# Keeping the last 32 tokens' gates on the chip and re-pacing the gathers, one-hots and u blocks of a PEER block

## The chip, the core and the metric

The kernel runs on one NeuronCore of a Trainium2 chip. The engines work side by side, each through its own instruction queue in program order, and wait for one another by semaphores: PE multiplies matrices, DVE (VectorE) and ACT (ScalarE) do elementwise work, POOL (GpSimd) does elementwise work and issues gathers, SP issues DMA. The metric is device microseconds (us) of one launch, lower is better.

## The reference, cut to what matters

```python
h2  = rmsnorm(x, g_ffn)                                  # 512 tokens of 1024
q   = (h2 @ w_q).reshape(T, 8, 2, 128)                   # 8 heads, two halves
s   = einsum('thpc,hpkc->thpk', q, sub_keys)             # 128 keys for each half
top_s, top_i = top_k(s, 16)                              # best 16 of each half
cand = top_s[:, :, 0, :, None] + top_s[:, :, 1, None, :] # their sums
fin_s, pos = top_k(cand, 16);  idx = 128 * i + j of the winners
gates = softmax(fin_s)
act = gelu(einsum('thkd,td->thk', expert_u[idx], h2))    # 128 experts of each token
x   = x + einsum('thk,thkd->td', gates * act, expert_v[idx])
out = rmsnorm(x, g_final)
```

Ahead of this stand a token mixer (projections, pooling, a short convolution) and its residual, which the change doesn't touch.

## The kernel before, in words

All matrix products are float32 split into a high and a low half and three products (`mm3`, lines 57 to 60). A high half is a cast on ACT (`split`, line 54; `u_high`, line 430; `v_high`, line 826), a low half is a subtraction on DVE or POOL (lines 55, 434, 830).

- **Two ways to the experts.** 320 of the 512 tokens (TU) go densely: all 16384 experts are multiplied, as 128 blocks of 128 experts. The other 192 tokens gather their 128 experts' rows from HBM. Half a tile of tokens (TM = 64) gathers only u; a last tile of 128 tokens gathers u and v.
- **A u block** (`u_tick`, or its parts written out): load 128 experts' u (`ur`, SP), high half on ACT (`u_high`, for the block two further on), low half (`u_low`, POOL or DVE, the same block), 24 matmuls into `b` (`u_mm`), gelu on ACT into `a` (`u_act`, line 451), and for the first 75 blocks a store to HBM (`Ad`). Blocks run in all stages: in norm (U_NORM = 2), in routing (U_HEAD, by head, and U_GATE = 10 after the heads), in the build (48), after it (U_END = 4) and the rest in the v stage.
- **Routing.** For each of 8 heads: queries on PE, top 16 on DVE (`best_keys`), sums of candidates on POOL (`candidates`), top 16 of the sums (`best_sums`), one-hot comparisons (`best_pairs`), their products on POOL (`pair_mults`), sums (`pair_keys`). It ends in `key` and `gate`, transposed on PE into columns `cols` in the middle of a u block.
- **The build.** The gate matrix of every dense token (128 x 128 keys) is a product of two one-hot matrices. 48 iterations of 8 tokens: in each, `one_hots(n + 2)` and `one_hots(n + 3)` compare on DVE for the groups of 4 tokens of the next iteration; then come a u block, the copies of older results from PSUM to `stage` (`to_stage`, ACT), the low half `u_low(i + 2)` on DVE, the one-hot matmuls of groups n and n + 1, and after each group some gathered rows (`gather`). Of the one-hots, `oi` carries no gate and ACT multiplies it in (4 activations, line 769) for even groups; for odd groups DVE does comparison and gate in 4 `tensor_scalar` (line 773). A full stage of 32 tokens (2 MB) is written to HBM (`Gd`), 12 times.
- **Rows.** The gathers form one list (`plan`): 64 u rows of the half tile, then the last tile's u and v rows by chunks of 16. `gather(want, more)` uses rows up to number want on DVE (lines 711 and 718) and has POOL issue at most `more` further ones, at most LAG = 4 ahead. After the 16th u row of a chunk come a gelu on ACT and a product on POOL (line 716), and POOL's later gathers stand behind that product. R_BUILD = 0.93 is the number of rows for each group in the build.
- **After the build.** `a_load` and `g_load` bring activations and gates back from HBM, 4 expert blocks of gates at a time (`gt`). Four u blocks (k = 0 to 3) run; `weigh(0)` stands in the third. `weigh(i)` multiplies activations and gates on DVE (line 852) and splits them (`wH`, `wL`).
- **The v stage.** For each i, `v_mm(i)` (line 864) multiplies 128 experts' v with the weights, while `weigh(i + 1)`, the v halves of i + 2 and some rows go on; from i = 74 on each iteration has a u block too. The rows are spread by costs (1.25 without a u block, 3.4 with one) to end some iterations before the last.

The order in each queue is that of the code (`manual_schedule`).

Of the kernel before, what the change touches and what calls it, by code (L numbers as in the profile page):

```python
# [8 lines left out]
F32 = mybir.dt.float32  # L9
# [7 lines left out]
P = 128  # L17
D = 1024
# [5 lines left out]
NK = 128  # L24
# [6 lines left out]
TD = KD * P  # L31

TM = 64
TU = TD - TM

U_NORM, U_HEAD, U_GATE, U_END = 2, (1, 1, 2, 1, 2, 1, 2, 1), 10, 4

R_BUILD = 0.93

TG, IG = 32, 4  # L40

# [6 lines left out]
def block_kernel(ctx: ExitStack, tc: tile.TileContext, io, out, dbg=None):  # L48
    nc = tc.nc
# [14 lines left out]
    def bank(i, dt=F32):  # L64
        return psum.tile([P, 512], dt, tag=f"b{i}", name=f"b{i}")
# [7 lines left out]
    keep = ctx.enter_context(tc.tile_pool(name="keep", bufs=1))  # L73
# [78 lines left out]
    def norm(tb, g, dst=None):  # L152

        xg = dst if dst is not None else wpool.tile([P, D], F32, tag="xg", name="xg")
        st = rms_sum([x1[:, tb]], [xg])
        rms_sqrt(st)
        nc.vector.scalar_tensor_tensor(xg, x1[:, tb], rms_inv(st)[0], g, op0=ALU.mult, op1=ALU.mult)
        return xg
# [147 lines left out]
    for hf in range(2):  # L306
# [11 lines left out]
        for e in range(2):  # L318
# [6 lines left out]
            g = hf * 2 + e  # L325
# [7 lines left out]
        for e in range(2):  # L333
            zb = z_chunk(wb, e)
            p = fpool.tile([P, T], F32, tag="p", name="yb", bufs=2)
# [10 lines left out]
    for hf in range(4):  # L346
# [14 lines left out]
        for e in range(2):  # L361
# [4 lines left out]
            t = fpool.tile([P, T], F32, tag="s", name="t", bufs=2)  # L366
# [4 lines left out]

    nc.scalar.activation(warm, warm, AF.Sqrt)
    hn = keep.tile([P, NT - KD, D], F32, name="hn")
    hm = keep.tile([P, D], F32, name="hm") if TM else None
    h2H = keep.tile([P, DC, T], F32R, tag="hH", name="h2H")
    h2L = keep.tile([P, DC, T], F32R, tag="hL", name="h2L")

# [36 lines left out]
    n_ahead = U_NORM + sum(U_HEAD) + U_GATE + TD // 8 + U_END  # L414
    assert TM in (0, P // 2)
    dram = ctx.enter_context(tc.tile_pool(name="dram", bufs=1, space=bass.MemoryType.DRAM))
    Gd = dram.tile([TD // TG, P, NK, TG], F32, name="Gd")
    Ad = dram.tile([n_ahead, P, TU], F32, name="Ad")
    raws, us, hid = {}, {}, {}
    nu = [0]  # L420
# [1 line left out]
    def u_load(i):  # L422
        if i < NK:
            raws[i] = upool.tile([P, DC, P], F32, tag=f"ur{i % 3}", name="ur", bufs=1)
            nc.sync.dma_start(raws[i], io["expert_ut"][i])

    def u_high(i):
        if i < NK:
            us[i] = [upool.tile([P, DC, P], F32R, tag=f"u{x}{i % 3}", name=f"u{x}", bufs=1) for x in "HL"]
            nc.scalar.copy(us[i][0], raws[i])  # L430

    def u_low(i, eng):
        if i < NK:
            eng.tensor_tensor(us[i][1], raws.pop(i), f(us[i][0]), ALU.subtract)  # L434
# [5 lines left out]
    def u_mm(i, half=None):  # L440
        o = bank(i % 2)
        uH, uL = us.pop(i)
        for c in range(DC):
            if c == DC // 2 and half is not None:
                half()
            mm3(o[:, :TU], uH[:, c], uL[:, c], h2H[:, c, :TU], h2L[:, c, :TU], c == 0, c == DC - 1)
        return o

    def u_act(i, o):
        a = upool.tile([P, TU], F32, tag="a", name="a", bufs=3)  # L450
        nc.scalar.activation(a, o[:, :TU], AF.Gelu)  # L451
        if i < n_ahead:
            nc.scalar.dma_start(Ad[i], a)
        else:
            hid[i] = a

    def u_tick(n=1, eng=nc.gpsimd, half=None):
        for _ in range(n):
            i = nu[0]
            nu[0] += 1  # L460
            u_load(i + 3)
            u_high(i + 2)
            if eng is not None:
                u_low(i + 2, eng)
            u_act(i, u_mm(i, half))
# [16 lines left out]
    add_x(NT - 1, 1, o)  # L482
    norm_T(NT - 2, xgs[NT - 2], h2H, h2L, (bank(6), bank(7)))
    norm(NT - 1, gb2, hn[:, 0])
    u_tick()
    norm_T(NT - 1, hn[:, 0], h2H, h2L, (bank(6), bank(7)))
    u_tick(U_NORM - 1)
    if TM:

        for q in range(2):  # L490
# [99 lines left out]
    def pair_mults(h, eng=nc.gpsimd):  # L590
        full = [P, NT, TOPK, TOPK]
        for s in range(2):
            eq, tf = eqs[h, s]
            eng.tensor_tensor(eq, eq, tf[:, :, None, :].to_broadcast(full), ALU.mult)
# [20 lines left out]
            pair_mults(h - 1)  # L615
        w = w_next
    best_keys(q1, H - 1, 1)
    u_tick(2)
    pair_mults(H - 2)
    candidates(H - 1)  # L620
    u_tick()
# [12 lines left out]
    nc.vector.tensor_tensor(gate, gate, zs[:, :, :, None].to_broadcast([P, NT, H, TOPK]), ALU.mult)  # L634
    pair_mults(H - 1, nc.vector)
    pair_keys(H - 1)
    u_tick(U_GATE - 5)


    cols = [upool.tile([P, KD, P], F32, name=f"col{s}", bufs=1) for s in range(3)]  # L640
# [80 lines left out]
    def gather(want, more):  # L721

        gather_use(min(want, n_issue[0]))
        gather_issue(min(n_done[0] + LAG, n_issue[0] + more))
# [1 line left out]

    vpool = tc.alloc_tile_pool(name="vpool", bufs=3, reuse_waits="tile")
    opool = tc.alloc_tile_pool(name="opool", bufs=3, reuse_waits="tile")
    spool = tc.alloc_tile_pool(name="spool", bufs=2, side="right", reuse_waits="tile")
    vraw, vs, gts, ws, abs_ = {}, {}, {}, {}, {}  # L730

    def v_load(i):
# [4 lines left out]
    built, stages = {}, {}  # L737

    def to_stage(n):

        t1 = 4 * n % TG
        if t1 == 0:
            stages[0] = spool.tile([P, NK, TG], F32, tag="stage", name="stage")
        stage = stages[0]
        nc.scalar.copy(stage[:, :, t1:t1 + 4], built.pop(n).rearrange("p (t i) -> p i t", t=4))
        if t1 + 4 == TG:
            for q in range(2):
                ks = slice(q * 64, q * 64 + 64)
                nc.scalar.dma_start(Gd[4 * n // TG, :, ks], stage[:, ks])
# [3 lines left out]
    def one_hots(n):  # L753

        if n >= TD // 4:
            return
        tb, t0 = divmod(4 * n, P)
        oi, oj = (opool.tile([P, 4, P], F32, tag=x, name=x, bufs=4) for x in ("oi", "oj"))
        full = [P, 4, P]

        def compare(o, c):
            nc.vector.tensor_tensor(o, iota[:, None, :].to_broadcast(full), c[:, tb, t0:t0 + 4][:, :, None].to_broadcast(full),
                                    ALU.is_equal)

        compare(oi, cols[0])
        if n % 2 == 0:
            compare(oj, cols[1])
            for t in range(4):
                nc.scalar.activation(oi[:, t], oi[:, t], AF.Copy, scale=cols[2][:, tb, t0 + t:t0 + t + 1])
        else:  # L770
            for t in range(4):
                c1, c2 = (c[:, tb, t0 + t:t0 + t + 1] for c in cols[1:])
                nc.vector.tensor_scalar(oj[:, t], iota, c1, c2, op0=ALU.is_equal, op1=ALU.mult)
        hot[n] = (oi, oj)
# [5 lines left out]
    for n in range(0, TD // 4, 2):  # L780
        left = TD // 4 - n
        if TM and left == TM // 4 + 6:

            assert n_done[0] >= TM
            ms_ = mdots[:, TM:2 * TM]
            nc.scalar.activation(ms_, ms_, AF.Gelu)
            nc.vector.tensor_tensor(ms_, ms_, mgate, ALU.mult)
        if TM and left == TM // 4 + 2:

            b = bank(2 + (n + 2) % 6)  # L790
            for q in range(2):
                nc.tensor.matmul(b[:, :TM], mdots[:, (1 - q) * TM:(1 - q) * TM + P], ident[:, q * TM:(q + 1) * TM],
                                 start=q == 0, stop=q == 1)
            nc.scalar.copy(cols[2][:, KD - 1, P - TM:], b[:, :TM])
        one_hots(n + 2)
        one_hots(n + 3)
        i = nu[0]
        nu[0] += 1
        u_load(i + 3)
        u_high(i + 2)  # L800
        if n:
            to_stage(n - 2)
            to_stage(n - 1)
        u_act(i, u_mm(i))
        u_low(i + 2, nc.vector)
        if 24 <= left < 30:
            v_load((28 - left) // 2)
        for g in (n, n + 1):
            oi, oj = hot.pop(g)
            b = bank(2 + g % 6)  # L810
            for t in range(4):
                nc.tensor.matmul(b[:, t * P:(t + 1) * P], oj[:, t], oi[:, t], start=True, stop=True)
            built[g] = b
            gather(int((g + 1) * R_BUILD), 2)
    to_stage(TD // 4 - 2)
    to_stage(TD // 4 - 1)
    opool.release()
# [3 lines left out]
    epool = tc.alloc_tile_pool(name="epool", bufs=2, reuse_waits="tile")  # L821
# [10 lines left out]
    def g_load(i):  # L832
        if i < NK:
            if i % IG == 0:
                gt = epool.tile([P, TD // TG, IG, TG], F32, tag="gt", name="gt")
                nc.sync.dma_start(gt.rearrange("p n i t -> p n (i t)"),
                                  Gd[:, :, i:i + IG, :].rearrange("n j i t -> j n (i t)"))
                for k in range(IG):
                    gts[i + k] = gt[:, :, k]

    def a_load(i):
        if i < n_ahead:
            abs_[i] = epool.tile([P, TU], F32, tag="ab", name="ab", bufs=3)
            nc.sync.dma_start(abs_[i], Ad[i])
# [24 lines left out]
            v_part(i, tb)  # L869
        del ws[i], vs[i]  # L870

    gfin = epool.tile([P, D], F32, name="gfin", bufs=1)

    def add_acc(tb, hf):
        cs = slice(hf * 512, (hf + 1) * 512)
# [24 lines left out]
    acc = [[bank(2 + 2 * tb + hf) for hf in range(2)] for tb in range(KD)]  # L900
    a_load(0)
    a_load(1)
    for k in range(U_END):
        u_tick(1, nc.vector)
        gather(n_issue[0], 2)
        if k == 0:
            v_high(0)
            v_low(0)
        if k == 1:
            g_load(0)  # L910
            v_high(1)
            v_low(1)
        if k == U_END - 2:
            weigh(0)
# [58 lines left out]
    vpool.release()  # L973
    gpool.release()
    upool.release()


# ---- launch: one core; inputs as the reference has them, without the leading axis of one layer
# [38 lines left out]
```

## Time and profile before

| what | value |
|---|---|
| time, 3 runs | median 1573.53 us (1570.72 to 1574.1) |
| the profiled execution's own time | 1573.27 us |
| its span (first to last instruction) | 1571.5 us |
| busy: PE, DVE, ACT, POOL | 1483.9 (94%), 1241.7 (79%), 625.8 (40%), 715.7 (46%) us |
| mean granted clock of TensorE | 0.980 |
| DMA | 419.57 MB, 267 GB/s over the span |

The span is 1.8 us shorter than the time of the same execution; sums over spans are therefore added to 1573.27 us. The stages by the trace: mixer to 293, norm to about 312, routing to 503, build 508 to 800, the four u blocks and the first v blocks to 850, v stage without u blocks to 1157, with them to 1535, then the last norm. Times in rows are us from the span's start.

### The profile page before, as it was taken

What the parts mean: (1) busy time and instruction counts of PE and PEld (TensorE: products, weight loads), DVE (VectorE), ACT (ScalarE), POOL (GpSimd) and SP (SyncE); (2) the same over time, 40 slices, a digit from 0 to 9 for tenths busy, and PEclk for the clock granted to TensorE, in tenths of its full rate; (3) what the DMA queues carried; (4) which work ended last, traced back from release to release, by engine and by line L of the source; (5) the groups of instructions that cost most, each with busy time, mean ns of one, the idle gap of its engine ahead of it and who ended that gap; (6) DMA issues with size and microseconds to landing.
All of it is one profiled execution on the core that took longest, in us unless ns stands there. A gap on an engine that the chain in (4) does not pass through costs nothing. (4 is left out here: it accounts for less than half of the span.)

```text
span 1571.5 us, 22106 instructions
## 1 busy us (share of the span) xinstructions
PE 1483.9 (94%) x7953; PEld 1304.4 (83%) x7953; DVE 1241.7 (79%) x2455; ACT 625.8 (40%) x1016; POOL 715.7 (46%) x448
## 2 busy tenths in 40 slices
PE   8999999899997989888967999999999999999997
PEld 6788888788897988888966887887789999999996
DVE  6832334559999999999977888887788989898985
ACT  4222222433334555555542333333334333333344
POOL 3433222247777433333344444443355666566620
PEclk9999999999998999999998999999999999999999
DMA  5222234422224999999899999999999999999971
GB/s 181 88 87 82 92 108 161 153 92 107 80 93 140 346 337 374 333 366 381 324 392 350 342 358 338 360 352 319 332 366 336 370 378 361 374 364 356 360 282 67
DMA packets 167452, 419.57 MB, mean 267 GB/s; under 512 B 13744, under 2 KB 84144, under 8 KB 160688
## 3 DMA queue, kind: packets, MB, share of 16 engines
q1 hardware_dynamic: 106944, 212.92, 38.4%
q0 software_dynamic: 46144, 167.80, 28.2%
q10 hardware_dynamic: 14256, 37.46, 6.4%
q8 instruction: 62, 1.02, 0.2%
q14 instruction: 46, 0.38, 0.1%
HBM read 377.99 MB, written 39.55 MB: 266 GB/s over the span
## 5 line engine op out<-in xcount | busy, mean ns | idle before, releaser
L58 PE MATMUL b<-h2H,uH 128*128 128x320 f32 x1024 | 327.3, 320 | 29.8 <-ACT a L451 29.5
L60 PE MATMUL b<-h2H,uL 128*128 128x320 f32 x1024 | 321.2, 314 | 12.1 <-POOL uL L434 6.6
L59 PE MATMUL b<-h2L,uH 128*128 128x320 f32 x1024 | 321.0, 314 | 1.0 <-DVE h2L L55 1.0
L699 POOL DMA_INDIRECT gr<-in_expert_u,gidx x128 | 204.2, 1595 | 187.7 <-DVE dots L711 108.4
L699 POOL DMA_INDIRECT gr<-in_expert_v,gidx x128 | 189.8, 1483 | 144.9 <-DVE x L718 102.2
L864 PE MATMUL b<-vH,wH 128*128 128x512 f32 x768 | 242.0, 396 | 13.8 <-ACT wH L54 13.8
L864 PE MATMUL b<-vL,wH 128*128 128x512 f32 x768 | 239.2, 392 | 0.0
L864 PE MATMUL b<-vH,wL 128*128 128x512 f32 x768 | 239.0, 392 | 0.0
L58 PEld LDWEIGHTS b<-h2H,uH 128*128 128x128 f32 x1024 | 197.3, 193 | 36.6 <-ACT a L451 34.0
L60 PEld LDWEIGHTS b<-h2H,uL 128*128 128x128 f32 x1024 | 196.8, 192 | 13.0 <-POOL uL L434 6.8
L59 PEld LDWEIGHTS b<-h2L,uH 128*128 128x128 f32 x1024 | 197.0, 192 | 3.2 <-DVE h2L L55 1.2
L54 ACT CAST wH<-gt 128x384 fp32r<-128x384 f32 x128 | 65.7, 513 | 300.7 <-DVE gt L852 296.5
L864 PEld LDWEIGHTS b<-vH,wH 128*128 128x128 f32 x768 | 142.7, 190 | 44.9 <-ACT wH L54 19.7
L718 DVE SCALAR_TENSOR_TENSOR x<-gr,dots,x 128x1024 f32<-128x1024 f32 x128 | 164.0, 1281 | 15.0 <-DMA gr<-in_expert_v,gidx 13.2
L864 PEld LDWEIGHTS b<-vL,wH 128*128 128x128 f32 x768 | 145.5, 189 | 31.2
L864 PEld LDWEIGHTS b<-vH,wL 128*128 128x128 f32 x768 | 145.4, 189 | 30.7
L830 DVE TENSOR_TENSOR vL<-vr,vH 128x1024 fp32r<-128x1024 f32 x128 | 156.5, 1223 | 16.5 <-ACT vH L826 13.7
L826 ACT CAST vH<-vr 128x1024 fp32r<-128x1024 f32 x128 | 134.6, 1051 | 81.2 <-PE b L864 74.8
L711 DVE CUSTOM_DVE_ANT_0 gr<-gr,hn 128x1024 f32<-128x1024 f32 x128 | 152.3, 1219 | 9.2 <-DMA gr<-in_expert_u,gidx 9.1
L55 POOL TENSOR_TENSOR wl<-raw,wh 128x2048 fp32r<-128x2048 f32 (+1 forms) x21 | 79.3, 3775 | 156.0 <-ACT wh L54 156.0
L699 POOL DMA_INDIRECT gr<-in_expert_u,midx x64 | 82.4, 1288 | 124.9 <-DVE mdots L711 111.9
L430 ACT CAST uH<-ur 128x1024 fp32r<-128x1024 f32 x128 | 133.1, 1040 | 14.9 <-DMA ur<-in_expert_ut 9.4
(215 smaller groups left out, 2526.8 us busy)
## 6 DMA issues: line engine op xcount, KB each, us to landing
ur<-in_expert_ut SPq DMA_DIRECT2D x128, 512.0 KB, 7.1
vr<-in_expert_v SPq DMA_DIRECT2D x128, 512.0 KB, 6.7
Gd<-stage ACTq DMA_DIRECT2D x24, 1024.0 KB, 8.9
gt<-Gd SPq DMA_DIRECT2D x32, 768.0 KB, 10.0
raw<-in_w_in SPq DMA_DIRECT2D x15, 1024.0 KB, 4.8
Ad<-a ACTq DMA_DIRECT2D x75, 160.0 KB, 6.0
ab<-Ad SPq DMA_DIRECT2D x75, 160.0 KB, 7.9
raw<-in_w_q SPq DMA_DIRECT2D x8, 1024.0 KB, 8.7
```

Source lines behind the costliest of these rows:

```text
L54: nc.scalar.copy(Hd, src)
L55: (nc.gpsimd if pool else nc.vector).tensor_tensor(Ld, src, f(Hd), ALU.subtract)
L58: nc.tensor.matmul(o, lh, rh, start=first, stop=False)
L59: nc.tensor.matmul(o, lh, rl, start=False, stop=False)
L60: nc.tensor.matmul(o, ll, rh, start=False, stop=last)
L430: nc.scalar.copy(us[i][0], raws[i])
L699: nc.gpsimd.indirect_dma_start(out=r, out_offset=None, in_=io["expert_u" if kind == "u" else "expert_v"], in_offset=bass.IndirectOffsetOnA ...
L711: nc.vector.tensor_tensor_reduce(out=r, in0=r, in1=src, op0=ALU.mult, op1=ALU.add, scale=1.0, scalar=0.0, accum_out=dst)
L718: nc.vector.scalar_tensor_tensor(x1[:, KD + g], r, dots[:, g, k:k + 1], x1[:, KD + g], op0=ALU.mult, op1=ALU.add)
L826: nc.scalar.copy(vs[i][0], vraw[i])
L830: nc.vector.tensor_tensor(vs[i][1], vraw.pop(i), f(vs[i][0]), ALU.subtract)
L864: nc.tensor.matmul(acc[tb][hf], lw[:, ts], rw[:, hf * 512:(hf + 1) * 512], start=i == 0 and rw is vH and lw is wH, stop=last and i == NK - 1)
```

## The change

1. Odd groups n with n % 4 = 1 now also leave the gate to ACT (two comparisons on DVE, 4 activations on ACT). Only n % 4 = 3 keeps the 4 `tensor_scalar`.
2. From row 64 on the build takes rows at R_LATE = 0.4 for each group, not 0.93.
3. The last stage of 32 tokens (of 12) isn't written to HBM. It stays in its own pool to the end; `g_load` loads 11 chunks (704 KB, not 768) and ACT copies the twelfth. The final norm's weights take the memory of `hm`.
4. `g_load(0)` stands ahead of the four u blocks, not in the second.
5. In norm, both u blocks stand ahead of the last tile's transposes. After the heads, 4 blocks stand ahead of `pair_mults(H - 2)` and `candidates(H - 1)`, not 2, and 3 at the end, not 5.

```diff
-R_BUILD = 0.93
+R_BUILD, R_LATE = 0.93, 0.4
...
-    Gd = dram.tile([TD // TG, P, NK, TG], F32, name="Gd")
+    Gd = dram.tile([TD // TG - 1, P, NK, TG], F32, name="Gd")
...
     norm(NT - 1, gb2, hn[:, 0])
-    u_tick()
+    u_tick(U_NORM)
     norm_T(NT - 1, hn[:, 0], h2H, h2L, (bank(6), bank(7)))
-    u_tick(U_NORM - 1)
...
     best_keys(q1, H - 1, 1)
-    u_tick(2)
+    u_tick(4)
     pair_mults(H - 2)
     candidates(H - 1)
     u_tick()
...
-    u_tick(U_GATE - 5)
+    u_tick(U_GATE - 7)
...
-        if t1 + 4 == TG:
+        if t1 + 4 == TG and 4 * n // TG < NG - 1:
             for q in range(2):
                 ks = slice(q * 64, q * 64 + 64)
                 nc.scalar.dma_start(Gd[4 * n // TG, :, ks], stage[:, ks])
...
-        if n % 2 == 0:
+        if n % 4 != 3:
             compare(oj, cols[1])
             for t in range(4):
                 nc.scalar.activation(oi[:, t], oi[:, t], AF.Copy, scale=cols[2][:, tb, t0 + t:t0 + t + 1])
...
-            gather(int((g + 1) * R_BUILD), 2)
+            gather(int(min((g + 1) * R_BUILD, TM + max(0, g + 1 - TM / R_BUILD) * R_LATE)), 2)
...
-                gt = epool.tile([P, TD // TG, IG, TG], F32, tag="gt", name="gt")
-                nc.sync.dma_start(gt.rearrange("p n i t -> p n (i t)"),
+                gt = epool.tile([P, NG, IG, TG], F32, tag="gt", name="gt")
+                nc.sync.dma_start(gt[:, :NG - 1].rearrange("p n i t -> p n (i t)"),
                                   Gd[:, :, i:i + IG, :].rearrange("n j i t -> j n (i t)"))
+                nc.scalar.copy(gt[:, NG - 1], stages[0][:, i:i + IG])
...
     a_load(1)
+    g_load(0)
     for k in range(U_END):
         u_tick(1, nc.vector)
         gather(n_issue[0], 2)
...
         if k == 1:
-            g_load(0)
```

**ACT in the build, two iterations before.** `oi` scaled by line 769 belongs to a group's one-hots, `uH` is the high half of the u block two further on, `b` to `stage` the copies from PSUM.

```order
L769 ACTIVATE oi<-oi,col_4159 128x128 x4
L430 CAST uH<-ur 128x1024
L745 COPY stage<-b_4846 128x128x4
L745 COPY stage<-b_4854 128x128x4
L451 ACTIVATE a<-b_4885 128x320
L453 DMA Ad<-a 128x320
L769 ACTIVATE oi<-oi,col_4159 128x128 x4
```

Now, at the same place:

```order
L771 ACTIVATE oi<-oi,col_4159 128x128 x8
L430 CAST uH<-ur 128x1024
L747 COPY stage<-b_4854 128x128x4
L747 COPY stage<-b_4862 128x128x4
L451 ACTIVATE a<-b_4894 128x320
L453 DMA Ad<-a 128x320
L771 ACTIVATE oi<-oi,col_4159 128x128 x4
```

In every second iteration 8 activations stand ahead of the cast `uH` where 4 stood; in the other ones nothing moved.

**DVE in the build now**, in such an iteration: the low half `uL` reads that `uH`, and the rows (line 710 now, 711 before) stand behind it.

```order
L764 TENSOR_TENSOR oi<-iota,col_4157 128x512
L764 TENSOR_TENSOR oj<-iota,col_4158 128x512
L764 TENSOR_TENSOR oi<-iota,col_4157 128x512
L764 TENSOR_TENSOR oj<-iota,col_4158 128x512
L434 TENSOR_TENSOR uL<-ur,uH 128x1024
L710 ISA gr,mdots<-gr,hm 128x1024
```

Before, the fourth of these was `L773 TENSOR_SCALAR oj<-iota,col_4158,col_4159 128x128 x4`; `uL` stands at the same place behind it.

**SP after the build, before and now**: the loads of activations (`ab`), of u (`ur`) and of gates (`gt`).

```order
L844 DMA ab<-Ad 128x320 x2
L425 DMA ur<-in_expert_ut 128x1024 x2
L836 DMA gt<-Gd 128x12x128
L425 DMA ur<-in_expert_ut 128x1024 x2
L916 DMA gfin<-in_g_final 128x1024
```

```order
L847 DMA ab<-Ad 128x320 x2
L838 DMA gt<-Gd 128x11x128
L425 DMA ur<-in_expert_ut 128x1024 x4
L919 DMA gfin<-in_g_final 128x1024
```

The gate load moved ahead of the first two u loads. On POOL, after the heads, the low halves `uL` that stand ahead of `pair_mults(H - 2)` and `candidates(H - 1)` are two more, and two fewer stand behind them.

## Rows read from the trace of the kernel before

**Rows 1.** Stages: window, length, busy PE, PEld, DVE, ACT, POOL, clock, DMA, GB/s

```profile
312.00:503.00 191.00, 179.64 (x1007) 160.83 (x1006) 169.16 (x879) 67.57 (x100) 131.81 (x81) 0.97 0.29 103
508.00:800.00 292.00, 263.67 (x1907) 259.35 (x1905) 288.81 (x549) 165.05 (x375) 117.23 (x91) 0.98 0.95 352
...
851.00:1157.00 306.00, 300.03 (x1307) 244.76 (x1307) 248.04 (x330) 113.34 (x148) 129.35 (x80) 0.99 0.97 342
1157.00:1535.00 378.00, 378.00 (x2084) 342.45 (x2083) 332.11 (x403) 144.48 (x208) 214.20 (x140) 1.00 0.95 353
```

**Rows 2.** Waits of PE: total us, times, longest

```profile
PE b L58 <- ACT a L451: 29.5, 23, 5.9
...
PE b L60 <- POOL uL L434: 6.6, 1, 6.6
```

**Rows 3.** Timeline of DVE, one build iteration (start, us, operation)

```profile
597.19 0.69 DVE L762 TENSOR_TENSOR oi<-iota,col 128x512 f32<-128x512 f32 x1
...
599.02 1.10 DVE L773 TENSOR_SCALAR oj<-iota,col,col 128x128 f32<-128x128 f32 x4
600.15 1.23 DVE L434 TENSOR_TENSOR uL<-ur,uH 128x1024 fp32r<-128x1024 f32 x1
601.30 1.22 DVE L711 CUSTOM_DVE_ANT_0 gr<-gr,hm 128x1024 f32<-128x1024 f32 x1
```

**Rows 4.** Timeline of ACT, the same iteration

```profile
597.91 1.28 ACT L769 ACTIVATE oi<-oi,col 128x128 f32<-128x128 f32 x4 [2.89 <-DVE oi L762]
599.09 1.03 ACT L430 CAST uH<-ur 128x1024 fp32r<-128x1024 f32 x1
```

**Rows 5.** Timeline of PE: first and last group of the last build iteration

```profile
794.61 0.41 PE L58 MATMUL b<-h2H,uH 128*128 128x320 f32 x1
...
798.24 1.97 PE L812 MATMUL b<-oi,oj 128*128 128x128 f32 x16
```

**Rows 6.** Timelines of DVE, POOL and PE in norm

```profile
300.32 2.27 DVE L147 TENSOR_TENSOR st<-st 128x1 f32<-128x1 f32 x1
...
300.22 2.34 POOL L434 TENSOR_TENSOR uL<-ur,uH 128x1024 fp32r<-128x1024 f32 x1
...
304.43 1.94 PE L166 MATMUL b<-ident,hn 128*128 128x128 f32 x8 [3.88 <-DVE hn L157]
```

**Rows 7.** Timelines of POOL and DVE at the end of routing

```profile
468.81 5.53 POOL L594 TENSOR_TENSOR eq<-eq,tf 128x1024 f32<-128x1024 f32 x2 [3.94 <-DVE eq L584]
474.30 1.17 POOL L551 TENSOR_TENSOR cand<-tv 128x128 f32<-128x128 f32 x4
...
475.50 0.67 DVE L514 MAX8 fv<-cand 128x8 f32<-128x80 f32 x4 [1.02 <-POOL cand L551]
...
495.92 4.56 DVE L594 TENSOR_TENSOR eq<-eq,tf 128x1024 f32<-128x1024 f32 x2
```

**Rows 8.** Timelines after the build: ACT, SP, PE, DVE, POOL

```profile
806.07 1.06 ACT L430 CAST uH<-ur 128x1024 fp32r<-128x1024 f32 x1 [0.89 <-ACT stage L745]
817.45 1.05 ACT L430 CAST uH<-ur 128x1024 fp32r<-128x1024 f32 x1 [8.54 <-DMA ur<-in_expert_ut]
...
814.86 0.38 SPq L836 DMA_DIRECT2D gt<-Gd  x1
...
818.88 0.63 PE L58 MATMUL b<-h2H,uH 128*128 128x320 f32 x1 [5.91 <-ACT a L451]
...
828.85 1.21 DVE L711 CUSTOM_DVE_ANT_0 gr<-gr,hn 128x1024 f32<-128x1024 f32 x1
...
831.50 1.05 POOL L699 DMA_INDIRECT gr<-in_expert_v,gidx  x1
...
838.10 1.28 DVE L718 SCALAR_TENSOR_TENSOR x<-gr,dots,x 128x1024 f32<-128x1024 f32 x1 [3.65 <-DMA gr<-in_expert_v,gidx]
...
843.35 1.22 PE L864 MATMUL b<-vH,wH 128*128 128x512 f32 x2 [5.30 <-ACT wH L54]
```

**Rows 9.** Granted clock while the second v block starts (columns as in rows 1)

```profile
843.00:849.00 6.00, 5.65 (x13) 4.46 (x14) 5.05 (x6) 1.76 (x3) 1.84 (x2) 0.51 0.98 328
```

More of the change, by code (lines that the diff above doesn't have):

```diff
@@ L373, in block_kernel @@
     hn = keep.tile([P, NT - KD, D], F32, name="hn")
-    hm = keep.tile([P, D], F32, name="hm") if TM else None
+    hm = keep.tile([P, D], F32, tag="hm", name="hm")
     h2H = keep.tile([P, DC, T], F32R, tag="hH", name="h2H")
@@ L728, in block_kernel @@
     opool = tc.alloc_tile_pool(name="opool", bufs=3, reuse_waits="tile")
-    spool = tc.alloc_tile_pool(name="spool", bufs=2, side="right", reuse_waits="tile")
+    lpool = tc.alloc_tile_pool(name="lpool", bufs=1, side="right", reuse_waits="tile")
+    spool = tc.alloc_tile_pool(name="spool", bufs=1, side="right", reuse_waits="tile")
+    NG = TD // TG
     vraw, vs, gts, ws, abs_ = {}, {}, {}, {}, {}
@@ L742, in to_stage @@
         if t1 == 0:
-            stages[0] = spool.tile([P, NK, TG], F32, tag="stage", name="stage")
+            stages[0] = (lpool if (4 * n // TG) % 2 == (NG - 1) % 2 else spool).tile([P, NK, TG], F32, tag="stage", name="stage")
         stage = stages[0]
         nc.scalar.copy(stage[:, :, t1:t1 + 4], built.pop(n).rearrange("p (t i) -> p i t", t=4))
-        if t1 + 4 == TG:
+        if t1 + 4 == TG and 4 * n // TG < NG - 1:
             for q in range(2):
@@ L870, in v_mm @@
         del ws[i], vs[i]
-    gfin = epool.tile([P, D], F32, name="gfin", bufs=1)
+    gfin = keep.tile([P, D], F32, tag="hm", name="gfin")
     def add_acc(tb, hf):
@@ L975, in block_kernel @@
     upool.release()
+    lpool.release()
 _SHAPES = {
```

## The prediction

> **What bounds the kernel now.** I read the busy times by stage first [rows 1]. The reader is to see which engine has no slack where. In routing and above all in the build it is DVE: 288.8 of the build's 292 us, while PE has 263.7. In the v stage it is PE: 300.0 of 306 us, then 378.0 of 378, with DVE at 81% and 88%. So a microsecond of DVE counts in full in the build, and in the v stage only when DVE is late by more than its slack. The waits of PE [rows 2] say the same: most of its idle time, 29.5 us, is a wait for an ACT gelu, and ACT itself is behind DVE.
>
> Then I read one build iteration on DVE and ACT side by side [rows 3, 4], because the change touches both. DVE compares from 597.19; three comparisons take 1.83 us (0.61 each), the four gated ones 1.13 (599.02 to 600.15). ACT starts its 4 gate activations at 597.91, as soon as the first comparison is there, and after 1.18 us casts `uH` (599.09 to 600.12). DVE's `uL` starts at 600.15. So two things end together there: DVE's own comparisons (600.13) and ACT's cast (600.12). `uL` needs both, and the rows stand behind it. After `uL` the next thing starts 1.15 us later, and a row costs 1.15 as well.
>
> **The change, part by part.** All times below are in the frame of the trace of before.
>
> *Odd groups to ACT.* DVE replaces 1.13 us by one comparison of 0.61 and saves 0.52. But ACT has a second group of 4 activations ahead of the cast: 1.18 us more, by the same row. The cast then ends at 599.09 + 1.18 + 1.03 = 601.30, and `uL` can't start before 601.33, where DVE would have been ready at 599.6. DVE stands for about 1.7 us, and the rows behind it with it. Net: +1.18 us in each such iteration. ACT can't start earlier, since its first activation waits for DVE's first comparison of the same iteration (2.89 us idle ahead of it). The affected iterations are n = 2, 6, ... 90: 23. Sum +27.1 us; between 23 (if 0.18 of it hides) and 29.4 (if the full 1.28 of a group counts).
>
> *Fewer rows late.* At the end of iteration n = 90 (92 groups) before wants 0.93 * 92 = 85 rows, the change 64 + 0.4 * (92 - 68.8) = 73. That takes 12 * 1.15 = 13.8 us from DVE. Does PE allow it? One iteration of PE lasts 3.63 us of u block and 1.97 of one-hots [rows 5], 5.6, a pair 11.2. DVE's late pair is 2.98 + 1.15 and 4.16 + 1.15 with 0.8 rows each, 11.3. So DVE still decides, barely. Build in sum: +27.1 - 13.8 = **+13.3 us** (+9 to +16).
>
> *Norm.* PE stands 3.88 us ahead of the last transposes [rows 6], waiting for `hn`. The second u block, 3.63 us, now fills this. But its low half on POOL now comes right behind the one that ends at 302.56. The rows show what that does: a 1-element DVE product took 2.27 us, from 300.32 to the very end of POOL's operation. Two operations that make `hn` stand behind it, and would wait some 2.3 us once more. So of at most 4.7 us (the gap and about a microsecond of clock behind it), none to all is won: **-2**. Routing starts that much earlier, and as DVE bounds routing it ends that much earlier.
>
> *Four u blocks ahead of `pair_mults`.* POOL idled for 3.94 us ahead of `pair_mults` [rows 7]. Two more low halves of 2.34 us don't fit in there, and the second must wait for a cast that follows another block's gelu: I count until about 471.8, so `pair_mults`, 468.81 before, start 3 us later, and `cand` too, at about 477.3. DVE, which waited 1.02 us for it, waits about 4. Behind it two fewer low halves run against DVE's products; each can stretch one by 2.2 us (two products that take 2.3 us alone took 4.56 at 495.92), but the moved ones now meet the comparisons ahead of `pair_mults`. I take **+2.8** (0 to +5). PE's wait of 6.6 us [rows 2] goes, but wins nothing: the ten blocks are the same ten, and PE now waits longer for the keys.
>
> *After the build.* This is where the load of gates hurts now [rows 8]. Let T0 = 800.2 be the end of the last one-hots (798.24 + 1.97). The gate load stands at 814.86, behind a 2 MB write; an u load came 8.54 us late, PE waited 5.91 at 818.88, and the second v block starts at T0 + 43.1, at a granted clock of 0.51 [rows 9], the 1.2 GHz level: about 2.9 us more. In all 46.
> Now: no write, so `uH` of k = 0 (806.07, T0 + 5.9) comes at about T0 + 5.3 and its `uL` at + 6.4. DVE has from there: that `uL`, 4 rows, a v half, `uL`, 2 rows: 9 * 1.15 = 10.4, end at + 16.7. The second of these 2 rows is number 80, the 16th of a chunk. Behind it stand gelu, product and two gathers, which the next two rows need ahead of `weigh(0)`. That is the stall that before has at 828.85: row, product, gather at 831.50, next row at 838.10, 8.1 us after the chunk's last row ended; with two rows some 11. So `weigh(0)` comes at + 27.8, the first v block at about + 29, with a cold start of 7 us; the second at + 36. Gain **-10** (-5 to -16: less if the rows' gathers are late, most if they aren't).
>
> *V stage.* 15 more rows are left, 15 * 1.22 = 18 us of DVE, in 684 us where DVE has 104 us free: hidden but for iterations with two rows, which get more frequent; PE loses there 6 of 306 us now. One ACT copy for every 4 blocks (0.3 us by the activations of [rows 4]) is hidden: ACT is busy for 38%. The DMA gets 15 * 0.5 MB more and 30 * 64 KB less. I take **+2** (-1 to +7).
>
> Sum: 13.3 - 2 + 2.8 - 10 + 2 = +6.1 us. The profiled execution took 1573.27 us, 0.3 below the median of the runs, so **1579 us**. A difference under 0.2%, 3.1 us, is about what can't be told from none.
>
> **The rivals.**
>
> *ACT's second group is free and the build gets shorter.* Then DVE wins 0.52 us in 17 early pairs, 8.8 us, and the late part runs at PE's 5.6 us, 12 iterations in 67 instead of 74.5 us: 16 us less, with the other terms 1573.3 - 16 - 2 + 2.8 - 10 + 2 = 1550. For it: ACT is busy for only 165 of the build's 292 us [rows 1]. Against it: these are not idle where they are needed; the cast ends when `uL` starts, to 0.03 us [rows 3, 4]. It decides if `uL` in the changed kernel starts less than 3 us behind the first comparison. Chance 0.12. (The Trainium skill, Perfetto Trace Analysis, section Optimizing Scalar/DVE Operations, says that work may well go from DVE to ScalarE where DVE is saturated. By that rule this rival's 1550 would come out; the trace has the saturated DVE, 289 of 292 us, but shows a chain through both engines as well.)
>
> *The end gives back all that the build takes.* If rows and u loads arrive in time after the build, 16 us come back, and norm gives 4.7: 1573.3 + 13.3 - 4.7 + 2.8 - 16 + 2 = 1571, no change. For it: the write of 2 MB is gone, and the late build asks for fewer gathers. Chance 0.16.
>
> *The gate load isn't what held the v blocks.* Rows behind the chunk's product hold `weigh(0)`, which before were behind it. If that eats all but 3 us: 1586. For it: the second v block waited for just that in before (838.10). Chance 0.15.
>
> *The DMA of the v stage is full.* Its share is 0.95 to 0.97 [rows 1]; 5.6 MB more at 350 GB/s are 16 us if nothing hides them: 1593. Against it: PE has no idle time from 1157 on at that share. Chance 0.07.
>
> **How the numbers follow.** My forecast has 0.50, its own range is 1574 to 1585. The range of 1567 to 1590 leaves out the first and the last rival, 0.19. Slower by over 0.2%: most of the forecast (0.40), the third and the fourth rival, 0.62. Within 0.2%: the lower end of the forecast (0.10) and most of the second rival, 0.21. Faster: the first rival and the rest of the second, 0.17.
>
> **What would show it.** In the build, DVE waits for ACT's `uH` ahead of `uL`, some 40 us over 23 waits, with PE idle longer; the last one-hots end some 14 us later. Ahead of the columns PE waits about 10 us for keys, where it waited for POOL. PE stands some 10 us ahead of the first v block, not ahead of the second. I am wrong if `uL` doesn't wait, if the v blocks start much sooner after the one-hots than 29 us, or if PE gets idle time beyond 1157.

## The result, and the profile after

The changed kernel takes 1587.96 us (median of 4 runs, 1586.04 to 1590.25), the kernel before 1572.12 beside it (1569.1 to 1574.1): ratio 1.0103, 95% interval 1.008 to 1.0126. It is slower, by 1.0%. The profiled execution after is the longest of the four, 1590.25 us with a span of 1588.5, 17.0 more than the span before.

The stages after, columns as in [rows 1]: the build, the v stage without u blocks, and the v stage with them in two parts.

```profile
508.00:820.00 312.00, 272.94 (x1919) 266.41 (x1918) 266.03 (x455) 196.24 (x477) 97.39 (x78) 0.97 0.89 317
861.00:1168.00 307.00, 299.43 (x1310) 243.47 (x1309) 254.21 (x344) 116.36 (x166) 140.21 (x88) 1.00 0.99 349
1168.00:1313.00 145.00, 145.00 (x802) 131.36 (x801) 128.96 (x165) 56.30 (x82) 89.45 (x60) 1.00 0.99 368
1313.00:1552.00 239.00, 234.36 (x1276) 209.71 (x1275) 213.28 (x250) 87.22 (x138) 136.43 (x89) 1.00 0.94 350
```

DVE was busy for all but 3 us of the build; now it idles for 46 of 312 us. And in the v stage, where PE had not a microsecond of idle time from 1157 on, it now has 4.6 in the last part.

The waits of PE, as in [rows 2]:

```profile
PE b L58 <- ACT a L451: 35.6, 29, 2.1
PE b L867 <- ACT wH L54: 23.4, 21, 11.3
PE b L645 <- DVE key L597: 7.8, 2, 7.6
...
PE b L60 <- POOL uL L434: 3.9, 1, 3.9
```

One build iteration on DVE, and the same on ACT, as in [rows 3, 4]:

```profile
598.10 0.69 DVE L764 TENSOR_TENSOR oi<-iota,col 128x512 f32<-128x512 f32 x1
...
599.94 0.68 DVE L764 TENSOR_TENSOR oj<-iota,col 128x512 f32<-128x512 f32 x1
602.30 1.23 DVE L434 TENSOR_TENSOR uL<-ur,uH 128x1024 fp32r<-128x1024 f32 x1 [1.68 <-ACT uH L430]
...
598.82 2.51 ACT L771 ACTIVATE oi<-oi,col 128x128 f32<-128x128 f32 x8 [1.68 <-DVE oi L764]
601.24 1.03 ACT L430 CAST uH<-ur 128x1024 fp32r<-128x1024 f32 x1
```

DVE is through with its comparisons at 600.62 and stands until 602.30, because ACT first does eight gate activations (2.4 us) and then the cast. `uL` starts 4.20 us behind the first comparison, where it started 2.96 behind it before.

Behind the build (DVE, PE, SP), as in [rows 8]:

```profile
842.06 1.23 DVE L710 CUSTOM_DVE_ANT_0 gr<-gr,hn 128x1024 f32<-128x1024 f32 x1 [3.15 <-DMA gr<-in_expert_u,gidx]
...
832.17 0.41 PE L58 MATMUL b<-h2H,uH 128*128 128x320 f32 x1 [1.04 <-ACT a L451]
...
847.88 1.22 PE L867 MATMUL b<-vH,wH 128*128 128x512 f32 x2 [11.29 <-ACT wH L54]
...
822.08 1.66 SPq L425 DMA_DIRECT2D ur<-in_expert_ut  x2
```

The clock while the first v block starts, as in [rows 9]:

```profile
848.00:854.00 6.00, 6.00 (x17) 4.76 (x18) 5.47 (x8) 2.26 (x4) 2.35 (x3) 0.61 0.87 327
```

The u loads hardly hold PE now: its longest waits in the four u blocks are 1.04 and 0.36 us, where they were 5.91 and 4.64. (ACT's cast at 830.74 still stood idle for 4.06; the u load issued at 822.08 landed at 830.66.) PE's gap stands ahead of the first v block, with two rows (842.06 is the first) ahead of `weigh(0)` that are late. After this gap of 11.29 us the granted clock is 0.61 for 6 us, nearer the 1.2 GHz level than the 2.4, so the cold start has only moved.

DVE in the late v stage, one whole iteration:

```profile
1403.33 1.22 DVE L434 TENSOR_TENSOR uL<-ur,uH 128x1024 fp32r<-128x1024 f32 x1
1404.47 0.48 DVE L855 TENSOR_TENSOR gt<-a,gt 128x320 f32<-128x320 f32 x1
1405.53 0.56 DVE L55 TENSOR_TENSOR wL<-gt,wH 128x384 fp32r<-128x384 f32 x1 [0.58 <-ACT wH L54]
1406.01 5.24 DVE L717 SCALAR_TENSOR_TENSOR x<-gr,dots,x 128x1024 f32<-128x1024 f32 x4
1411.16 1.22 DVE L832 TENSOR_TENSOR vL<-vr,vH 128x1024 fp32r<-128x1024 f32 x1
1412.30 1.22 DVE L434 TENSOR_TENSOR uL<-ur,uH 128x1024 fp32r<-128x1024 f32 x1
...
1414.97 3.92 DVE L717 SCALAR_TENSOR_TENSOR x<-gr,dots,x 128x1024 f32<-128x1024 f32 x3
...
1419.94 1.22 DVE L434 TENSOR_TENSOR uL<-ur,uH 128x1024 fp32r<-128x1024 f32 x1
```

From `uL` to `uL` this takes 8.97 us, with four rows. The next iteration has three and takes 7.64, and PE's iteration is 7.62 (the median distance from gelu to gelu there). So three v rows fill DVE, and a fourth takes 1.33 us more than PE's iteration has. Counted from `uL` to `uL` through both traces, 9 iterations have four rows here, and none in before.

### The profile page after: what moved, and what is told of

It is laid out like the page before. It is cut to its first block, busy times and chain, and to the rows that moved or that the text cites. A ratio compares the mean times of both kernels' runs of the same rounds, so it can differ in the third digit from the quotient of the medians.

```text
span 1588.5 us, 22139 instructions
## 1 busy us (share of the span) xinstructions
PE 1490.4 (94%) x7953; PEld 1304.8 (82%) x7953; DVE 1234.6 (78%) x2383; ACT 657.4 (41%) x1144; POOL 715.3 (45%) x448
## 5 line engine op out<-in xcount | busy, mean ns | idle before, releaser
L698 POOL DMA_INDIRECT gr<-in_expert_u,gidx x128 | 198.3, 1549 | 205.0 <-DVE dots L710 136.6
L698 POOL DMA_INDIRECT gr<-in_expert_v,gidx x128 | 198.4, 1550 | 136.2 <-DVE x L717 90.5
L832 DVE TENSOR_TENSOR vL<-vr,vH 128x1024 fp32r<-128x1024 f32 x128 | 156.3, 1221 | 17.7 <-ACT vH L828 15.7
L434 DVE TENSOR_TENSOR uL<-ur,uH 128x1024 fp32r<-128x1024 f32 x105 | 128.1, 1221 | 48.9 <-ACT uH L430 48.0
```

The source lines that it names most:

```text
L698: nc.gpsimd.indirect_dma_start(out=r, out_offset=None, in_=io["expert_u" if kind == "u" else "expert_v"], in_offset=bass.IndirectOffsetOnA ...
L832: nc.vector.tensor_tensor(vs[i][1], vraw.pop(i), f(vs[i][0]), ALU.subtract)
```

## The experiments

Three rounds each, if nothing else is said (4 to 12 timed executions). To see where each run gains, I follow one row through all traces: ACT's gelu (line 451), which stands at 706.56 (early build), 803.26 (last block of the build), 1181.66 (early in the v stage with u blocks) and 1550.94 (its end) in before. The table shows by how much the same row is later; the starts of the build alone differ by up to some 2 us from before. These columns compare single executions, and the one of before (1573.27) was 1 to 4 us slower than the medians of before beside the other kernels. So a gain by rows can be larger than by medians: fewer rows alone have -9.2 at 1551, and -4.5 by medians.

| kernel | median us | ratio to before (95%) | 707 | 803 | 1182 | 1551 |
|---|---|---|---|---|---|---|
| changed kernel | 1587.96 | 1.0103 (1.008 to 1.0126) | 20.6 | 18.4 | 9.6 | 16.9 |
| odd groups on DVE | 1562.91 | 0.9952 (0.9934 to 0.997) | -1.5 | -10.1 | -16.3 | -10.2 |
| before, odd groups on ACT | 1593.49 | 1.0167 (1.0144 to 1.019) | 16.9 | 25.4 | 18.7 | 18.7 |
| cast first | 1552.73 | 0.9893 (0.9876 to 0.9911) | -9.3 | -17.6 | -26.4 | -18.0 |
| weigh first | 1587.0 | 1.0119 (1.0096 to 1.0141) | 17.7 | 13.2 | 8.3 | 14.0 |
| no fourth row | 1581.09 | 1.0073 (1.0046 to 1.0099) | 17.7 | 14.1 | 6.5 | 7.9 |
| old places of u blocks | 1588.04 | 1.0107 (1.0089 to 1.0125) | 18.5 | 15.0 | 6.4 | 13.5 |
| before, gates' part alone | 1566.88 | 0.9972 (0.9957 to 0.9987) | -1.2 | -1.0 | -3.8 | -3.8 |
| before, fewer rows alone | 1565.41 | 0.9973 (0.9959 to 0.9987) | -1.3 | -9.4 | -15.7 | -9.2 |
| gates' part, load later | 1563.7 | 0.9955 (0.9939 to 0.9971) | -1.8 | -1.9 | -12.5 | -12.5 |
| cast first, row between | 1537.18 | 0.9788 (0.9766 to 0.981) | -12.7 | -24.0 | -37.3 | -37.3 |
| the same, fewer rows early | 1541.78 | 0.9822 (0.9797 to 0.9847) | -16.6 | -24.5 | -33.0 | -33.0 |
| the same, no hidden loads | 1535.94 | 0.9796 (0.9764 to 0.9828) | -18.3 | -26.1 | -39.3 | -39.3 |

### The odd groups: alone, undone, and with another order on ACT

**Undone in the changed kernel.**

```diff
-        if n % 4 != 3:
+        if n % 2 == 0:
```

> The changed kernel with the gates of all odd groups back on DVE; all else stays. The theory (the second group of activations ahead of the cast made DVE wait): the 23 waits of uL for uH in the build go, the late build with its fewer rows runs at PE's 5.6 us an iteration, so the last one-hots end some 7 us earlier than in before, and with the end (-12.7 by the two traces) and the v stage (+9.6) as in the changed kernel the time is about 1563 (1559 to 1568). The rival (the wait has another cause, such as the long issue of the gate stores on ACT): uL still waits for uH, and the time is 1575 to 1588.

1562.91: as the theory said. The 24 waits of `uL` for `uH` in the build of the changed kernel (44.4 us in all, most of them 1.68) are two short ones here, 1.4 us in all. DVE in such an iteration:

```profile
597.53 1.11 DVE L775 TENSOR_SCALAR oj<-iota,col,col 128x128 f32<-128x128 f32 x4
598.67 1.23 DVE L434 TENSOR_TENSOR uL<-ur,uH 128x1024 fp32r<-128x1024 f32 x1
```

**Alone, in the kernel of before** (the same line the other way).

> The kernel of before with only the odd groups' gates moved to ACT. The theory: 23 waits of about 1.7 us, net 1.18 each, +27 in the build, with ACT's store issues on top up to +31, nothing given back behind it: 1600 (1595 to 1606). The rival on record (ACT's second group is free): 1564. A third case: later stages give a part back, 1585 to 1594.

1593.49. The build loses 25.4 us, and 6.7 of them come back by 1182: the third case, with the theory's price in the build. ACT's second group is not free. The wait is the same one:

```profile
612.31 1.23 DVE L434 TENSOR_TENSOR uL<-ur,uH 128x1024 fp32r<-128x1024 f32 x1 [1.68 <-ACT uH L430]
```

**Another order on ACT, in the changed kernel.**

```diff
-        one_hots(n + 2)
-        one_hots(n + 3)
         i = nu[0]
         nu[0] += 1
         u_load(i + 3)
         u_high(i + 2)
+        one_hots(n + 2)
+        one_hots(n + 3)
```

> The changed kernel with the cast of the next u block ahead of the gates' activations on ACT, where it fits into ACT's 2.9 us of idle time ahead of the first comparison; nothing is taken back from ACT. The theory (the order on ACT, not its load, is what costs): uL no longer waits, the early pairs win 0.52 us each, the late part runs at PE's 5.6, the build ends 16 us before that of the old kernel: 1553 (1549 to 1560). The rival (ACT simply has too much work in an iteration, or the u block isn't loaded so early): the wait moves to PE's one-hots, which wait for oi, or to the cast, and the time stays at 1575 to 1588.

1552.73. The same work stays on ACT, and 35 us go. DVE and ACT there:

```profile
600.23 0.68 DVE L764 TENSOR_TENSOR oj<-iota,col 128x512 f32<-128x512 f32 x1
600.83 1.22 DVE L434 TENSOR_TENSOR uL<-ur,uH 128x1024 fp32r<-128x1024 f32 x1
...
596.97 1.05 ACT L430 CAST uH<-ur 128x1024 fp32r<-128x1024 f32 x1 [0.40 <-ACT a L451]
599.14 2.48 ACT L771 ACTIVATE oi<-oi,col 128x128 f32<-128x128 f32 x8 [1.12 <-DVE mdots L710]
```

The cast is over at 598.0, and `uL` follows DVE's comparisons without a wait. The gates' activations now end behind it, and nobody is late for that. So the 1550 of the rival on record was to be had; the order on ACT, not its load, stood against it. With the rest as in the changed kernel, the odd groups on ACT cost 25 us with the cast behind them (1587.96 against 1562.91 on DVE) and gain 10 with the cast ahead (1552.73). The cast ahead with the odd groups on DVE wasn't run; as `uL` waits for 1.4 us in all there, little of the 10 can be the order's alone.

### Behind the build: the gate load, the rows, `weigh(0)`

**`weigh(0)` earlier**, at the end of k = 1, in the changed kernel.

> The changed kernel with the first product with the gates, weigh(0), ahead of the rows of the third u block behind the build. The theory (PE's 11.3 us ahead of the first v block are the rows 842 and 846 that wait for the chunk's product, with weigh(0) behind them): the first v block starts some 8 us sooner, 1580 (1577 to 1584). The rival: the rows still stand ahead of the second weigh, so that the second v block waits for the same and less than 3 us are won: 1585 to 1588.

1587.0: the rival. The first and the second v block:

```profile
834.75 0.73 PE L867 MATMUL b<-vH,wH 128*128 128x512 f32 x2 [2.18 <-ACT wH L54]
...
848.71 1.22 PE L867 MATMUL b<-vH,wH 128*128 128x512 f32 x2 [9.56 <-ACT wH L54]
```

The first came 13 us sooner (10.7 sooner counted from the last one-hots, 818.2 here), and the gap moved to the second, which waits for the same rows.

**The gates' part alone, in the kernel of before**: the last 32 tokens' gates stay on the chip, and `g_load(0)` stands ahead of the u blocks.

> The kernel of before with only this part of the change: the last 32 tokens' gates stay on the chip, and the first load of gates stands ahead of the four u blocks. The theory (that load held up the u loads and the second v block): some 10 to 16 us less behind the build, nothing given back, since as many rows are done in the build as before: 1559 (1554 to 1565). The rival on record (the gate load isn't what held the v blocks, the rows do): at most 3 us, 1567 to 1571.

1566.88: outside the theory's range, and 0.1 us from the rival's. It gains 0.28%, where 0.8% was expected. The rows show why (ACT, SP, PE):

```profile
819.93 1.04 ACT L430 CAST uH<-ur 128x1024 fp32r<-128x1024 f32 x1 [12.70 <-DMA ur<-in_expert_ut]
...
800.41 0.40 SPq L839 DMA_DIRECT2D gt<-Gd  x1
801.20 9.49 SPq L425 DMA_DIRECT2D ur<-in_expert_ut  x3
801.20 6.76 SPq L425 DMA_DIRECT2D ur<-in_expert_ut  x1
...
821.37 0.64 PE L58 MATMUL b<-h2H,uH 128*128 128x320 f32 x1 [10.56 <-ACT a L451]
```

The last line of SP is the first of the same three loads by itself. With the load of gates ahead of them, the u loads come 12.70 us late; in before it was 8.54 [rows 8]. The write is gone, and the wait is not.

**The same with the first gate load behind the second u load, as in before** (5 rounds).

> The kernel with the gates' part alone (1567), with the first load of gates back behind the second u block, as in before; the last 32 tokens' gates still stay on the chip. The theory (ahead of the u loads the gate load itself makes them late: uH waited 12.7 us in that run, 8.5 in before): the u loads come in time, the v blocks start earlier: 1562 (1558 to 1565). The rival (the queue is full of gathers then, the place in it decides nothing): 1565 to 1569. A third case, the load behind them is what the first v block waits for: 1568 to 1572.

1563.7: the theory's direction, at the upper half of its range. Its `uH` waited 3.44 us instead of 12.70, and the trace gains 10.6 between 803 and 1182 instead of 2.8. By the medians the two differ by 3 us, by the traces by 9: the profiled execution of this kernel (span 1559.1) lies near the lower end of its times, that of the other (1567.8) at the upper end. The intervals of the two ratios overlap, so the times alone don't tell these kernels apart; the rows do, for the wait. PE still waits 5.53 us for a `uL` at 817.04: its u load is now the one directly behind the gate load, and took 5.78 us to issue.

**The fewer rows alone, in the kernel of before** (5 rounds; R_LATE as in the change).

> The kernel of before with only the fewer rows late in the build; gates as in before, all of them written and loaded again. With the gates alone (1567), both together with the odd groups on DVE (1563) and before (1571.6) this fills a table of two by two. One theory (the rows' gathers held up the u loads behind the build, so that fewer of them give the gain there by themselves): build -7.5, behind it -9, v stage +8: 1563 (1560 to 1566). The rival (each needs the other: the gates' load still waits for their write): build -7.5, behind it 0 to -3, v stage +8: 1569 to 1573.

1565.41, in the first theory's range. The gates are still written, and their load stands where it was. SP and PE there:

```profile
795.63 0.85 SPq L425 DMA_DIRECT2D ur<-in_expert_ut  x2
...
804.87 0.38 SPq L836 DMA_DIRECT2D gt<-Gd  x1
...
822.56 1.22 PE L864 MATMUL b<-vH,wH 128*128 128x512 f32 x2 [12.77 <-ACT wH L54]
```

Two u loads are issued in 0.85 us and come in time, and PE's gap is the same single one ahead of the first v block as in the changed kernel. The gain between 803 and 1182 is 6.3; with both parts (odd groups on DVE) it is 6.2. So by the rows the fewer rows give it alone (the gates' part with its load behind the u loads has 10.6), and both together give no more. The kernels also differ in how many rows are left for the early v stage, so these gains aren't of one cause alone.

### Norm and routing

**The u blocks back in their old places, in the changed kernel** (5 rounds).

> The changed kernel with the u blocks of norm and routing where they were. By the prediction (norm -2, routing +2.8) this gives 0.8: 1587. By the two traces the two moves together are worth -0.3 at the keys: 1588. The rival (the waits that they fill, 3.9 and 6.6 us, were worth something): 1591 to 1596.

1588.04, no difference. In the changed kernel's trace the two waits that these blocks were to fill have these successors:

```profile
306.26 1.73 PE L166 MATMUL b<-ident,hn 128*128 128x128 f32 x8 [2.36 <-DVE hn L157]
...
501.37 0.90 PE L645 MATMUL b<-ident,key 128*128 128x128 f32 x3 [7.60 <-DVE key L597]
```

In norm `hn` came 1.8 us later than in [rows 6]. In routing PE does its blocks sooner and then waits for the keys.

### The v stage

**No fourth row.** In the late v stage DVE skips what would be the fourth row of an iteration, so part of the gathered tokens' sum is left out.

```diff
...
-        for k in range(n_done[0], want):
+        first = n_done[0]
+        for k in range(first, want):
+            skip[0] = both and k - first >= 3
             gather(k + 1, 2)
```

> The changed kernel in which DVE leaves out every row that would be the fourth in an iteration of the late v stage (9 of 236 rows); the rows are still gathered, so the DMA does the same. Part of the gathered tokens' sum is left out for it. The theory (an iteration with three rows is already full on DVE, 7.64 us of PE's 7.62, and each fourth row costs 1.3): the second half of the v stage gets back what it lost, 7 us: 1581 (1578 to 1584). The rival on record (the DMA is full in the v stage): nothing changes, 1586 to 1590.

1581.09, 6.9 us less. From 1182 on 1.4 us are lost, where it was 7.3. The stretch from 1320 to 1500 in the changed kernel and here, columns as in [rows 1]:

```profile
1320.00:1500.00 180.00, 177.51 (x971) 159.12 (x970) 162.34 (x196) 63.34 (x98) 113.90 (x76) 1.00 0.99 370
```

```profile
1320.00:1500.00 180.00, 179.11 (x987) 161.95 (x986) 158.46 (x192) 65.90 (x99) 114.52 (x79) 1.00 0.99 373
```

The DMA is as busy as before (0.99), so the full DMA was not the cause of those 6 us.

**A row between**, on top of the cast first.

```diff
...
-            split(wH.rearrange("p (n t) -> p n t", t=TG), wL.rearrange("p (n t) -> p n t", t=TG), g)
+            h, l = (x.rearrange("p (n t) -> p n t", t=TG) for x in (wH, wL))
+            nc.scalar.copy(h, g)
+            if between is not None:
+                between()
+            nc.vector.tensor_tensor(l, g, f(h), ALU.subtract)
...
-        weigh(i + 1)
+        weigh(i + 1, lambda: gather(min(n_done[0] + 1, want), 2))
```

> The kernel with the cast first (1553), and in the v stage one row between the product with the gates and the low half of the weights, where DVE waits 0.58 us for ACT's cast in each iteration. The theory (DVE is full at three rows, so its own wait counts): 0.58 us for each of the 47 late iterations more than cover the 9 fourth rows' 1.3 us, so the late v stage loses nothing: 1545 (1542 to 1549). The rival (the DMA or the rows' gathers set the late v stage): 1551 to 1555.

1537.18: the theory's direction, and 5 us better than its range. It is 2.1% under before. DVE in an iteration with four rows:

```profile
1388.66 0.49 DVE L855 TENSOR_TENSOR gt<-a,gt 128x320 f32<-128x320 f32 x1 [0.57 <-ACT a L451]
1389.07 1.22 DVE L710 CUSTOM_DVE_ANT_0 gr<-gr,hn 128x1024 f32<-128x1024 f32 x1
1390.21 0.08 DVE L710 DVE_READ_ACCUMULATOR2_ANT dots<- 128x1 f32 x1
1390.21 0.55 DVE L862 TENSOR_TENSOR wL<-gt,wH 128x384 fp32r<-128x384 f32 x1
```

`wL` no longer waits, and DVE now waits for ACT's gelu: it has slack. From 1182 on nothing is lost (8.4 with the cast first alone). The early v stage gains too, 4.5 us: 13.3 between 803 and 1182, against 8.8. That is 12.9 of the 15.5 us between the medians. The 6.4 us at 803 lie in or ahead of a build of the same code, and I can't say what they are; the execution profiled with the cast first alone was the slowest of its four (1555.37).

**Fewer rows early** (R_BUILD 0.87), on top of that.

> The kernel with the cast first and a row between (1537), with 0.87 rows a group in place of 0.93 in the early build. The theory (the early build is still bound by DVE at 6.0 us an iteration against PE's 5.6, while the v stage now has slack for rows): some 4 rows of 1.15 us less early, two more rows in the v stage at no cost: 1533 (1530 to 1537). The rival (the v stage is full again, or PE is the bound in the build): 1537 to 1541.

1541.78: a miss. At 707 the row is 3.9 us earlier for it, but at 803 only 0.5, since the higher rate then lasts for more groups and only 2 rows fewer are done by the end of the build; and the early v stage became longer.

**The same without the loads of hidden values**, so that its sums are of other values.

> The kernel with fewer rows early (1542) in which the first three blocks' hidden values serve for all blocks whose values were stored, so that 72 loads of 160 KB are left out of the early v stage (11.8 MB of some 117 MB; the sums are then of other values). The theory (in the kernel with a row between, the early v stage is bound by the DMA, with a share of 0.97 to 1.01, so that an earlier start and more rows there come to nothing): the 7 us by which the early v stage got longer come back, and what PE still loses there: 1533 (1530 to 1536). The rival (fewer rows in the build cost something else, such as DVE in the v stage): 1539 to 1543.

1535.94, at the end of the theory's range. Stretch 812 to 1140, columns as in [rows 1], of the row between, of fewer rows early, and of this one:

```profile
812.00:1140.00 328.00, 324.01 (x1439) 265.34 (x1439) 272.45 (x371) 127.69 (x181) 110.01 (x97) 1.00 1.00 357
```

```profile
812.00:1140.00 328.00, 320.83 (x1409) 261.55 (x1409) 266.42 (x364) 124.98 (x177) 107.75 (x96) 0.99 0.98 352
```

```profile
812.00:1140.00 328.00, 323.99 (x1441) 265.31 (x1440) 270.46 (x369) 126.73 (x179) 111.01 (x97) 1.00 0.93 321
```

From 803 to 1182 it wins 13.2 us where the one before it won 8.5; PE is back at 324 of 328 us with the DMA at 0.93. So in the kernel with fewer rows early these loads cost the early v stage some 5 us. The share doesn't show it, for the kernel with the row between keeps PE at 324 at a share of 1.00. The waits of DVE for these loads in the same stretch do, in the row between and in fewer rows early:

```profile
DVE gt L855 <- DMA ab<-Ad: 4.2, 3, 1.9
```

```profile
DVE gt L855 <- DMA ab<-Ad: 8.9, 5, 3.0
```

Without the loads they are gone, and `gt` waits 4.7 us for the gates instead. Whether the loads are late because the DMA is full or because SP stands at their issue (below) isn't shown, nor why fewer rows early make more of them late.

## Why the prediction came out as it did

The direction was right (slower), and 1587.96 lies in the range of 1567 to 1590. But the forecast of 1579 was 9 us short, and the time lies outside the forecast's own range of 1574 to 1585, nearest to the third rival's 1586. That rival's reason didn't hold: most of the missing time was lost in the v stage, not behind the build. So the mechanism in the build was foreseen, and that the range held the end of the sum was in part luck.

**Odd groups to ACT, +27.1.** Right. Alone they cost 25.4 in the build. The step named the mechanism, a cast behind a second group of activations with DVE behind the cast, and the wait is the 1.68 that it worked out (about 1.7). The rule that the first rival cites (the Trainium skill, Perfetto Trace Analysis, section Optimizing Scalar/DVE Operations) says that offloading from a saturated DVE to ScalarE may pay. Here it didn't, by 25 us, until the cast went ahead; then the build was 17.6 us shorter than before. The build's gain is not all from ACT: with the odd groups on DVE it was 10.1 us shorter. The measurement decides: it depends on what stands behind the offloaded work on its new engine.

**Fewer rows late, -13.8, and the build, +13.3.** Right. In three kernels with the changed build (weigh first, no fourth row, old places) the last gelu of the build is 13.2 to 15.0 later. The profiled execution of the changed kernel had 18.4, and two of its gate stores held ACT up there. One of them, on ACT and then on DVE:

```profile
782.74 2.60 ACTq L751 DMA_DIRECT2D Gd<-stage  x2
785.44 0.44 ACT L451 ACTIVATE a<-b 128x320 f32<-128x320 f32 x1 [2.73 <-issue]
...
790.56 1.23 DVE L434 TENSOR_TENSOR uL<-ur,uH 128x1024 fp32r<-128x1024 f32 x1 [3.99 <-ACT uH L430]
```

The other took 2.36. The rest of its gate stores took 0.81 to 1.05, and `uL` mostly waits 1.68.

**Norm -2 and routing +2.8.** Their sum, +0.8, isn't told from nothing: the two runs differ by 0.1 us. The parts by themselves were read from one trace only; PE's wait for the keys (7.60, forecast about 10) came as the step said. Its wait for POOL's `uL` didn't go, but fell from 6.6 to 3.9.

**After the build, -10.** The size was right: from 803 to 1182 the changed kernel gains 8.8 us, with 1.6 more idle time of PE in the early v stage in it. From the last one-hots (820.6) to the first v block are 27.3 us (forecast 29), and the gap ahead of it is 11.3 (about 10). The cause was only half right. The step put it to the load of gates behind its write; the runs show that the fewer rows alone give it, and that the early load by itself brings the u loads later, not sooner. In the changed kernel, with both parts, PE's waits in the u blocks are 1.4 us in all.

**V stage, +2.** This is the step that failed in size: 1.6 in its early part (PE idles for 7.6 us, before 6.0), and 7.3 from 1182 on (9.6 to 16.9), about 9 in all, beyond the bound of +7. The sign that was named for it came: PE has idle time beyond 1157. The step counted 15 more rows against DVE's mean slack of 104 us. But the slack lies where it can't be used: an iteration with three v rows has none (7.64 us of 7.62). The 236 rows that are left for the v stage ask for four in 9 of the 47 late iterations, the 221 of before for four in none, and each fourth costs up to 1.3 us. Leaving these out returned 6.9 us between the medians. That is most of the 9 us that the forecast was short.

**The rivals.** The free second group didn't come. The end didn't give all back. The third (rows and not gates hold the v blocks) was right on the place of the wait, ahead of `weigh(0)`, but at no loss of the gain; that its 1586 comes nearest is chance. The full DMA wasn't it in the late v stage.

## What to carry to other kernels

Before work goes to an engine with idle time, look at what stands behind it there in program order and who waits for that; moving one short cast ahead turned a loss of 25 us into a gain of 10. Slack counts for each iteration, in whole pieces of work: a mean of 12% free didn't hold one more row of 1.3 us. And a short wait inside each iteration (0.58 us) is a place to put such a piece.

## What was not expected of the hardware

The issue of a load isn't always short, and the long ones stand directly behind a load of gates. In the kernel with the gates' part alone three u loads took SP 9.49 us, 6.76 of them the first; in the changed kernel, with its fewer rows, the first two behind the same load took 0.73 and 0.82 (the third waits 2.4 us for a `uL`, its issue takes 0.33), and with fewer rows and no gate load ahead two took 0.85 together. Through the trace of before from 795 on, 26 of the 32 loads that SP issues directly behind a load of gates took 1 us or more (up to 5.62), and 3 of the 260 others did. Without the loads of hidden values the next load comes some microseconds behind the gates', and from 812 to 1140 16 of 19 such issues took under 0.4. What an issue waits for isn't shown. On ACT the issue of a gate store took 2.60 and 2.36 where it is else 0.81 to 1.05, and there the engine's own work stood behind it.
